# S5 stage of a two-layer trunk on one core: half of the first tokens prepared inside the last GEMM, tile 0's outputs computed with channels on the partitions, gelus of tiles 2 and 3 apart, u gathered at odd steps

## The chip, the cores and the metric

One of the eight cores of a Trainium2 chip runs the whole program. The metric is the device time of one execution in microseconds, taken as the median over runs of the same kernel; smaller is better.

## What is computed

Two layers over 256 tokens of width 2048, in float32. The change lies in the mixer of the second layer, an S5 block, and at the end of the MLP ahead of it:

```python
def rmsnorm(x, g):
    y = xf * lax.rsqrt(jnp.mean(xf * xf, axis=-1, keepdims=True) + EPS)
    return y * g

def s5_mixer(h, ...):                 # 128 groups of 16 channels, 64 complex states each
    u = h.reshape(B, S, S5_GROUPS, S5_GROUP)
    ...
    bu_re = einsum('sgc,gpc->sgp', u_s, bb_re); bu_im = ...
    x_re, x_im = associative_scan(_scan_combine, (a, bu), axis=0)
    y = einsum('sgp,gcp->sgc', x_re, cr) - einsum('sgp,gcp->sgc', x_im, ci)
    y = y + d_skip * h
    g = gelu(y)
    val, gate = split(g @ w_glu, 2, axis=-1)
    return val * sigmoid(gate)

x = x + sqrelu_mlp(rmsnorm(x, norm_mlp[0]), ...)     # layer 0 ends
x = x + s5_mixer(rmsnorm(x, norm_mix[1]), ...)       # layer 1 begins
```

The factor of the rmsnorm of a token is known only when its whole row of x is there, so nothing of S5 that needs the factor can start before the last GEMM of the MLP has given that token's last 512 channels.

## The kernel before, in words

Every large product is a GEMM on TensorE (PE) in which 128x128 blocks of weights, or of the transposed activations, stand still and 512 columns stream past them. A weight chunk is loaded by the DMA queue of SyncE (SP), and ScalarE (ACT, line 191) and VectorE (DVE, line 113) split it into a high and a low part; three products of such parts make one.

The last GEMM ahead of S5 is `gemm_skewed` (line 299): its second half goes through the tokens 0 to 127 (t = 0) first and calls `done0` (line 1276) for them, then through the tokens 128 to 255 (t = 1) and calls it again. `done0` squares and sums the row (ACT) and gets the rstd of the 128 tokens (DVE and ACT, `Norm.finish`).

`s5_phase` (line 1129) works through 16 tiles j of 128 channels (8 groups). The 256 tokens are 64 chunks k of 4 tokens each. Per tile:

- u: `s5_u` (line 1022) brings two tiles at once into the layout that the next products want. TensorE writes the tokens transposed, and scaled by rstd, into a PSUM bank (line 1031), and 16 small ScalarE copies gather it (line 1036). Tiles 0 to 3 are gathered before the rstd is known and scaled later by `s5_scale` (line 1043). Their factor is a small product (line 1141) of two selection tables with the rstd.
- e: `s5_e` (line 1049) multiplies u with the input tables on TensorE (line 1056, 16 calls, each with 64 columns of weights), and VectorE turns the result by the phase tables, scans it over k (line 1066) and turns it back into the states X[j].
- y: `s5_y` (line 1078) sums u and the states into the outputs on TensorE (line 1089, 24 calls). ScalarE takes the gelu, 16 small instructions (line 1096) for one tile or, with twice the columns each, for a group of two, then casts the result (line 1100).
- glu: `glu_tile` (line 1116) multiplies the gelu of a tile with its rows of the GLU weights (line 1122), accumulating over tiles in four banks. It runs some tiles behind: tiles 0 and 1 at steps 2 and 3, tile i at step i + 3 after that (`LAG`).

Each engine runs its queue in the order in which the program names the instructions. In the loop over j that is: e of tile j+1, glu of an earlier tile, y of tile j, a ScalarE copy for the scan's decay (line 1020), the gelus when j ends a group, then, at j = 2, 4, 6, 8, u of the tiles j+6 and j+7. `keep_warm` (line 320) adds TensorE products whose result nobody reads (`WARM` = 18, 4 and 8 of them at three kinds of places).

The banks matter. In this stage e and u (from tile 8 on) share two PSUM banks in turn:

```python
cut(4)
rings["sd"], rings["y"] = [4, 5], [6, 7]
def bank():
    return ring("sd")      # s5_e, and s5_u with kind="sd"
```

A product that takes a bank waits until its last user, two calls back, has been read: an e by VectorE (line 107), a u by the last of ScalarE's 16 copies.

Of the kernel before, what the change touches and what calls it, by code (L numbers as in the profile page):

```python
# [38 lines left out]
Q = 4  # L39

SLOTS_HOP = 3
WARM = (18, 4, 8)
LAG = 3


# [12 lines left out]
def tile_trunk(  # L58
# [69 lines left out]
    def spawn(gen, delay=0):  # L128
        side.append([clock[0] + delay, gen])
# [892 lines left out]
    def s5_u(j, diag=None, kind="sd"):  # L1022

        ps = ring(kind).rearrange("p (i s) -> p i s", s=S)
        for i in range(2):
            for t in range(NT):
                o, xs = ps[:, i, t * P:(t + 1) * P], xres[t][:, (j + i) * P:(j + i + 1) * P]
                if diag is None:
                    pe.transpose(o, xs, ident)
                else:  # L1030
                    pe.matmul(o, xs, diag[:, t], start=True, stop=True)
        u = tmp([P, 2, Q, NCH], "vsb", bufs=4)
        pv = ps.rearrange("p i (k s) -> p i s k", s=L)
        for s in range(L):
            for q in range(Q):
                act.copy(u[32 * s:32 * s + 32, :, q], pv[32 * q:32 * q + 32, :, L - 1 - s])  # L1036
            yield s
        if diag is None:
            U[j] = u
        else:  # L1040
            U[j], U[j + 1] = u[:, 0], u[:, 1]

    def s5_scale(j, factor):
        u = U[j]
        uv = u.rearrange("p i q k -> p (i q) k")
        mult(uv, uv, factor[:, None, :].broadcast_to([P, 2 * Q, NCH]))
        U[j], U[j + 1] = u[:, 0], u[:, 1]

    def s5_e(j):
        te, to, tt, ct = tab[j]  # L1050
        u, dk, xp = U[j], dks[j % 4], xps[j % 4]
        pe_ = bank().rearrange("p (i q k) -> p i q k", i=2, q=Q)
        for i in range(2):
            for q in range(Q):
                for h in (slice(0, GP), slice(GP, P)):
                    pe.matmul(pe_[h, i, q], te[:, i, q, h], u[:, q], start=True, stop=True)
        sh = [P, 2, Q, NCH]
        tw = tmp([P, 2] + sh[1:], "c5")
        t1, t2 = tw[:, 0], tw[:, 1]
        mult(t1, pe_, ct[:, 0:1].broadcast_to(sh))  # L1060
        mult(t2, pe_, ct[:, 1:2].broadcast_to(sh))
        add(t1[:, 0], t1[:, 0], t2[:, 1])
        sub(t1[:, 1], t1[:, 1], t2[:, 0])
# [12 lines left out]
        X[j] = xp

    def s5_y(grp):

        n = len(grp)  # L1080
        py = ring("y").rearrange("p (j q k) -> p j q k", j=2, q=Q)
        for jj, j in enumerate(grp):
            te, to, tt, ct = tab[j]
            u, xp = U[j], X[j]
            for q in range(Q):
                terms = ((tt[:, q], u[:, q]), (to[:, 0, q], xp[:, 0, q]), (to[:, 1, q], xp[:, 1, q]))
                for m, (w_, d) in enumerate(terms):
# [28 lines left out]
    def glu_tile(j):  # L1116
# [3 lines left out]
        for i, accs in ((c, A["v"]), (c + 1, A["g"])):  # L1120
# [4 lines left out]
            if kk == WK - 1:  # L1125
                load_next()
                pos[0] += 1

    def s5_phase(norm):
# [3 lines left out]
        sel = wp.tile([P, 2, NT, P], F32, tag="wl", name="sel", bufs=LIVE)  # L1133
        ar, diag = sel[:, 0], sel[:, 1]
        for t in reversed(range(NT)):
            tsc(ar[:, t], sela.rearrange("p s r -> p (s r)"), norm.rstd[:, t:t + 1], ALU.mult)
        for t in range(NT):
            act.activation(diag[:, t], ident, AF.Copy, scale=norm.rstd[:, t:t + 1])
        prs = bank()[:, 0:NCH]
        for t in range(NT):  # L1140
            pe.matmul(prs, ar[:, t], selb[:, t], start=(t == 0), stop=(t == NT - 1))
        keep_warm(WARM[1])
        s5_scale(0, prs)
        s5_scale(2, prs)
        s5_e(0)
        for j in (4, 6):
            for _ in s5_u(j, diag, "acc"):
                pass
        groups = [(0,), (1,), (2, 3), (4, 5), (6, 7), (8, 9), (10, 11), (12, 13), (14,), (15,)]
        ys = {}  # L1150
        for grp in groups:
            gen = s5_y(grp)
            for j in grp:
                ys[j] = (gen, j == grp[-1])
        glu = 0
        for j in range(NJ):
            if j + 1 < NJ:
# [12 lines left out]
            if end:  # L1170
                for _ in gen:
                    pass
            if j in (2, 4, 6, 8):
                for _ in s5_u(j + 6, diag):
                    pass
            s5_fetch(j + 4)
            pump()
        while glu < NJ:
            prep(GLU0 + 16 + glu - NJ + LAG)
            glu_tile(glu)  # L1180
            glu += 1
        s5_rest(NJ)
# [212 lines left out]
```

## Time and profile before

| | |
|---|---|
| median of 3 runs | 2104.44 us (2101.5, 2104.44, 2106.57) |
| profiled execution, its own time | 2101.04 us |
| its span, first to last instruction | 2099.3 us |
| TensorE busy | 2076.1 us, 99% of the span |
| VectorE, ScalarE, GpSimd busy | 1369.1, 1061.4, 122.9 us |
| granted TensorE clock, mean | 0.999 |

The profile is one execution on the chip. A timeline row gives the start in us from the span's first instruction, the us from the first start to the last end of the merged instructions, the engine, the line of the kernel, the operation, the tiles (out<-in), shapes, the count, and in brackets how long the engine sat idle before and what ended it. Ends of matmuls are modelled, so the time that a product takes from the queue is read as the distance between two starts. An fp32 product shows as two matmul rows.

### The profile page before, as it was taken

How to read it: one execution, taken by the hardware profiler on the slowest of the kernel's cores; microseconds unless marked ns; L12 is line 12 of the kernel's file. 1: busy time of each engine (PE TensorE's matmuls, PEld its weight loads, DVE VectorE, ACT ScalarE, POOL GpSimd, SP SyncE). 2: the span in 40 equal slices, each digit the busy share in tenths (PEclk: the TensorE clock that was granted, in tenths of full speed). 3: DMA queues.
4: the chain of work that ended last, by engine and by line, in shares of the span. 5: the costliest groups of instructions: out<-in, count | busy, mean ns of one | idle time of the engine just before them, and what ended most of it. 6: DMA issues, size and time to landing. Idle time of an engine off the chain costs nothing.

```text
span 2099.3 us, 31788 instructions
## 1 busy us (share of the span) xinstructions
PE 2076.1 (99%) x12126; PEld 1763.8 (84%) x12126; DVE 1369.1 (65%) x2292; ACT 1061.4 (51%) x1640; POOL 122.9 (6%) x210
## 2 busy tenths in 40 slices
PE   8999999999999999999999999999999999999998
PEld 8899998888888888888887668888888888888886
DVE  5785656688678767767866865565556645645655
ACT  5545545555445444454566875444434434434443
POOL 2000200021021002100110000000000000000000
PEclk9999999999999999999999999999999999999999
DMA  7457765677776777687678765665565556555653
GB/s 244 157 193 241 248 178 184 214 229 267 237 240 233 273 238 222 225 276 235 208 266 310 274 215 187 200 201 199 189 195 189 189 193 191 178 204 181 200 192 131
DMA packets 230813, 452.57 MB, mean 216 GB/s; under 512 B 20818, under 2 KB 29348, under 8 KB 230660
## 3 DMA queue, kind: packets, MB, share of 16 engines
q1 hardware_dynamic: 217824, 415.29, 59.8%
q0 software_dynamic: 11440, 32.86, 4.9%
q10 hardware_dynamic: 1396, 2.39, 0.3%
q8 instruction: 95, 1.56, 0.3%
q14 instruction: 58, 0.48, 0.1%
HBM read 420.85 MB, written 41.68 MB: 220 GB/s over the span
## 4 chain that ended last, share of the span: by engine, by line
PE 91%; ACT 3%; DVE 3%; DMA 1%; issue 1%; SPq 0%; DVEq 0%; ACTq 0%
PE acc L265 21%; PE acc L201 15%; PE acc L202 15%; PE acc L203 15%; PE acc L269 11%; PE acc L1122 3%; PE acc L248 2%; PE acc L250 2%; PE acc L249 2%; DVE wl L113 1%; ACT wh L191 1%; PE y L1089 1%; ACT s2k L1096 1%; DMA raw<-in_a_w_in_dram 1%; ACT vsb L1036 1%
## 5 line engine op out<-in xcount | busy, mean ns | idle before, releaser
L113 DVE TENSOR_TENSOR wl<-raw,wh 128x1024 fp32r<-128x1024 f32 (+1 forms) x690 | 833.2, 1217 | 574.4 <-ACT wh L191 570.0
L191 ACT CAST wh<-raw 128x1024 fp32r<-128x1024 f32 (+1 forms) x690 | 712.9, 1047 | 631.0 <-PE acc L203 341.4
L201 PE MATMUL acc<-wh,x 128*128 128x512 f32 x832 | 326.8, 393 | 0.0
L203 PE MATMUL acc<-wh,x 128*128 128x512 f32 x832 | 324.0, 389 | 0.0
L202 PE MATMUL acc<-wl,x 128*128 128x512 f32 x832 | 324.0, 389 | 0.0
L265 PE MATMUL acc<-x,wh 128*128 128x512 f32 x1024 | 273.9, 394 | 2.8 <-DVE s2k L110 2.8
L265 PE MATMUL acc<-a,wh 128*128 128x512 f32 x1024 | 272.8, 393 | 0.0
L201 PE MATMUL acc<-wh,a 128*128 128x512 f32 x640 | 251.5, 393 | 0.0
L202 PE MATMUL acc<-wl,a 128*128 128x512 f32 x640 | 249.4, 390 | 0.1
L203 PE MATMUL acc<-wh,a 128*128 128x512 f32 x640 | 249.3, 390 | 0.0
L265 PEld LDWEIGHTS acc<-x,wh 128*128 128x128 f32 x1024 | 177.3, 189 | 28.9 <-DVE s2k L110 3.2
L265 PEld LDWEIGHTS acc<-a,wh 128*128 128x128 f32 x1024 | 177.3, 189 | 25.3 <-ACT s2k L1324 0.4
L203 PEld LDWEIGHTS acc<-wh,x 128*128 128x128 f32 x832 | 156.2, 188 | 32.9
L201 PEld LDWEIGHTS acc<-wh,x 128*128 128x128 f32 x832 | 156.3, 188 | 32.0 <-ACT vsb L1317 0.3
L202 PEld LDWEIGHTS acc<-wl,x 128*128 128x128 f32 x832 | 156.3, 188 | 31.8 <-issue 0.2
L269 PEld LDWEIGHTS acc<-a,wl 128*128 128x128 f32 x1024 | 152.8, 190 | 18.7
L269 PEld LDWEIGHTS acc<-x,wl 128*128 128x128 f32 x1024 | 152.4, 190 | 18.8
L269 PE MATMUL acc<-x,wl 128*128 128x256 f32 x1024 | 158.0, 282 | 0.0
L269 PE MATMUL acc<-a,wl 128*128 128x256 f32 x1024 | 157.5, 281 | 0.0
L248 PE MATMUL acc<-x,wh 128*128 128x256 f32 x512 | 148.4, 290 | 1.2 <-ACT wh L191 1.2
L249 PE MATMUL acc<-x,wh 128*128 128x256 f32 x512 | 145.4, 284 | 0.1
L250 PE MATMUL acc<-x,wl 128*128 128x256 f32 x512 | 145.5, 284 | 0.0
(246 smaller groups left out, 2105.8 us busy)
## 6 DMA issues: line engine op xcount, KB each, us to landing
raw<-in_mlp_w_dram SPq DMA_DIRECT2D x512, 512.0 KB
raw<-in_a_w_in_dram SPq DMA_DIRECT2D x94, 512.0 KB
raw<-in_b_w_glu_dram SPq DMA_DIRECT2D x64, 512.0 KB
raw<-in_a_w_out_dram SPq DMA_DIRECT2D x32, 512.0 KB
scr<-t POOLq DMA_DIRECT2D x32, 512.0 KB, 5.6
teo<-scr SPq DMA_DIRECT2D x32, 512.0 KB
t<-scr SPq DMA_DIRECT2D x16, 512.0 KB
pwr<-pwn SPq DMA_DIRECT2D x16, 256.0 KB
```

The lines of the kernel that those rows point to most:

```text
L113: v.tensor_tensor(out=o, in0=a, in1=b, op=ALU.subtract)
L191: act.copy(h[:, sl], r[:, sl])
L201: pe.matmul(accs[t], lhs.h[:, k, ts], wh, start=first, stop=False)
L202: pe.matmul(accs[t], lhs.h[:, k, ts], wl, start=False, stop=False)
L203: pe.matmul(accs[t], lhs.l[:, k, ts], wh, start=False, stop=last)
L248: pe.matmul(o, wh[:, kk, cs], lhs.h[:, k], start=f and c % 2 == 0, stop=False)
L249: pe.matmul(o, wh[:, kk, cs], lhs.l[:, k], start=False, stop=False)
L250: pe.matmul(o, wl[:, kk, cs], lhs.h[:, k], start=False, stop=e and c % 2 == 1)
L265: pe.matmul(a[c], wh, lhs.hl[:, k].rearrange("p i s -> p (i s)"), start=first, stop=False)
L269: pe.matmul(a[c][:, S:], wl, lhs.h[:, k], start=False, stop=last)
L1036: act.copy(u[32 * s:32 * s + 32, :, q], pv[32 * q:32 * q + 32, :, L - 1 - s])
L1122: pe.matmul(accs[t], g[:, t * P:(t + 1) * P], raws[i][:, kk], start=j == 0, stop=j == NJ - 1)
```

## The change

`s5_e` is cut into `s5_in` (TensorE), `s5_turn` and `s5_sums` (VectorE) and `s5_states` (VectorE), the first three of which can do half of the chunks k, that is the tokens of t = 0 or of t = 1. `s5_scale` can do halves too.

- The factor for t = 0 and the scaling of tiles 0 to 3 for it move into the last GEMM (`s5_ahead`, started when `done0` has the rstd of t = 0). After that GEMM's last product, ahead of the rstd of t = 1, come e's products of tiles 0 and 1 for t = 0, and tile 0's turn.
- `s5_phase` then does the other halves, for tile 0 ahead of the loop, for tile 1 at j = 0. `WARM` becomes (11, 2, 8).
- Tile 0's outputs come from `s5_y_direct`: the weights have 32 columns, each product writes 32 partitions, so that channels lie on the partitions and one ScalarE gelu takes the tile.
- Tiles 2 and 3 are groups of their own: 32 gelus on 64 columns instead of 16 on 128.
- u of the tiles 8 to 15 is gathered at the end of the steps j = 1, 3, 5, 7 instead of 2, 4, 6, 8.

```diff
-WARM = (18, 4, 8)
+WARM = (11, 2, 8)
...
+    def s5_in(j, ks=ALL):
+        te, u = tab[j][0], U[j]
+        pe_ = banks[j] = bank().rearrange("p (i q k) -> p i q k", i=2, q=Q)
         for i in range(2):
             for q in range(Q):
                 for h in (slice(0, GP), slice(GP, P)):
-                    pe.matmul(pe_[h, i, q], te[:, i, q, h], u[:, q], start=True, stop=True)
+                    pe.matmul(pe_[h, i, q, ks], te[:, i, q, h], u[:, q, ks], start=True, stop=True)
...
+    def s5_y_direct(j):
+        te, to, tt, ct = tab[j]
+        u, xp = U[j], X[j]
+        py = ring("y")[:, 0:S].rearrange("p (s k) -> p s k", s=L)
+        for s in range(L):
+            cs = slice(32 * s, 32 * s + 32)
+            for q in range(Q):
+                terms = ((tt[:, q], u[:, q]), (to[:, 0, q], xp[:, 0, q]), (to[:, 1, q], xp[:, 1, q]))
+                for m, (w_, d) in enumerate(terms):
+                    pe.matmul(py[32 * q:32 * q + 32, s], w_[:, cs], d, start=m == 0, stop=m == 2,
+                              tile_position=(0, 32 * q))
...
+        act.activation(g[:, 0].rearrange("p (k s) -> p s k", s=L), py, AF.Gelu_apprx_tanh)
...
+    def s5_ahead(norm):
+        yield from s5_factor(norm, 0)
+        s5_scale(0, prs[0], HALF[0])
+        s5_scale(2, prs[0], HALF[0])
...
+        for _ in s5_factor(norm, 1):
+            pass
+        s5_sums(0, HALF[0])
         keep_warm(WARM[1])
-        s5_scale(0, prs)
-        s5_scale(2, prs)
-        s5_e(0)
+        s5_scale(0, prs[0], HALF[1])
+        s5_in(0, HALF[1])
+        s5_turn(1, HALF[0])
+        s5_sums(1, HALF[0])
+        s5_scale(2, prs[0], HALF[1])
+        s5_turn(0, HALF[1])
+        s5_sums(0, HALF[1])
+        s5_states(0)
...
-        groups = [(0,), (1,), (2, 3), (4, 5), (6, 7), (8, 9), (10, 11), (12, 13), (14,), (15,)]
+        groups = [(0,), (1,), (2,), (3,), (4, 5), (6, 7), (8, 9), (10, 11), (12, 13), (14,), (15,)]
...
-            if j in (2, 4, 6, 8):
-                for _ in s5_u(j + 6, diag):
+            if j in (1, 3, 5, 7):
+                for _ in s5_u(j + 7, diag):
...
     def done0(u, ts):
         norm2.block(u, ts)
+        if u == NB - 1 and ts[0] == 1:
+            for j in range(2):
+                s5_in(j, HALF[0])
+            s5_turn(0, HALF[0])
```

The order of DMA issues on SP's queue stays the same, and so does GpSimd's.

First place, TensorE around u of the tiles 8 and 9 (the two L1031 rows on xres_76 and xres_77 are repeated once just ahead), before. `sd` is a bank of the pair, `teo_11850` holds the tables of tile 4, and `[waits ...]` names the engines and DMA queues that an instruction waits for.

```order
L1031 MATMUL sd_12014<-sel,xres_77 128x128
L1056 MATMUL sd_12041<-vsb_11726,teo_11850 64x64 [waits DMAHW5_49,DVE_49,PE_49]
L1056 MATMUL sd_12041<-vsb_11726,teo_11850 64x64 x15
L1122 MATMUL acc_11980<-raw_11498,s2k_11926 128x512 [waits Activation_49]
L1122 MATMUL acc_11981<-raw_11498,s2k_11926 128x512
L1122 MATMUL acc_11982<-raw_11516,s2k_11926 128x512
L1122 MATMUL acc_11983<-raw_11516,s2k_11926 128x512
```

The same place with the change; `teo_11899` holds the tables of tile 3.

```order
L1031 MATMUL sd_11988<-sel,xres_77 128x128
L1063 MATMUL sd_12015<-vsb_11233,teo_11899 64x64 [waits DMAHW0_49,DVE_49,PE_49]
L1063 MATMUL sd_12015<-vsb_11233,teo_11899 64x64 x15
L1170 MATMUL acc_12046<-raw_11498,s2k_11890 128x512 [waits DMAHW5_49,Activation_49]
L1170 MATMUL acc_12047<-raw_11498,s2k_11890 128x512
L1170 MATMUL acc_12048<-raw_11516,s2k_11890 128x512 [waits DMAHW6_49]
L1170 MATMUL acc_12049<-raw_11516,s2k_11890 128x512 [waits PE_49]
```

The u is followed by e of tile 3 now and by e of tile 4 before, so the next e, of tile 4, is the one that takes the bank of that u.

Second place, TensorE at e of tile 4 with the change: the last rows of y of tile 2 ahead, glu of tile 1 and the first row of y of tile 3 behind.

```order
L1114 MATMUL y_12054<-bc_11353,teo_11566 64x64 x4
L1063 MATMUL sd_12103<-vsb_11762,teo_11894 64x64 [waits DMAHW5_49,PE_49,Activation_49]
L1063 MATMUL sd_12103<-vsb_11762,teo_11894 64x64 x15
L1170 MATMUL acc_12046<-raw_11498,s2k_11970 128x512
L1170 MATMUL acc_12047<-raw_11498,s2k_11970 128x512
L1170 MATMUL acc_12048<-raw_11516,s2k_11970 128x512
L1170 MATMUL acc_12049<-raw_11516,s2k_11970 128x512
L1114 MATMUL y_12143<-vsb_11233,t_2137_11900 64x64 [waits DMAHW2_49]
```

Its wait for ScalarE ("Activation") is for the last copy of u of the tiles 8 and 9. The e of tiles 6, 8 and 10 have the same wait, for u of the tiles 10, 12 and 14; before, it stood at the e of tiles 5, 7, 9 and 11.

Third place, ScalarE from the gelus of tile 1 on, before (`s2k` is the gelu, `x` its cast, `s1k` the decay copy, `vsb` the gathered u):

```order
L1096 ACTIVATE s2k_11926<-y_11900 32x64 x16
L1100 CAST x_11848<-s2k_11926 128x256
L1020 COPY s1k_11352<-rr 128x4x63
L1036 COPY vsb_12019<-sd_12014 32x2x64 x16
L1020 COPY s1k_11356<-rr 128x4x63
L1096 ACTIVATE s2k_12106<-y_11988 32x128 x16
L1100 CAST x_11848<-s2k_12106 128x2x256
L1020 COPY s1k_11344<-rr 128x4x63
L1036 COPY vsb_12192<-sd_12187 32x2x64 x16
L1020 COPY s1k_11348<-rr 128x4x63
L1096 ACTIVATE s2k_12274<-y_12161 32x128 x16
L1100 CAST x_12291<-s2k_12274 128x2x256
```

With the change, from the gelus of tile 1 on:

```order
L1121 ACTIVATE s2k_11970<-y_11944 32x64 x16
L1125 CAST x_11892<-s2k_11970 128x256
L1036 COPY vsb_11993<-sd_11988 32x2x64 x16
L1020 COPY s1k_11352<-rr 128x4x63
L1121 ACTIVATE s2k_12080<-y_12054 32x64 x16
L1125 CAST x_11892<-s2k_12080 128x256
L1020 COPY s1k_11356<-rr 128x4x63
L1121 ACTIVATE s2k_12169<-y_12143 32x64 x16
L1125 CAST x_11892<-s2k_12169 128x256
L1036 COPY vsb_12192<-sd_12187 32x2x64 x16
L1020 COPY s1k_11344<-rr 128x4x63
L1020 COPY s1k_11348<-rr 128x4x63
```

The 16 copies of a u stood behind a decay copy, one step away from the gelus of a group; they now stand directly behind the gelus and the cast of the tile or group that ends at that step.

## Rows read from the trace of the kernel before

**Rows 1.** Timeline, TensorE, lead-in of S5 and its first steps.
```profile
1129.73 4.24 PE L326 MATMUL acc<-x 128*128 128x512 f32 x18
1133.81 0.55 PE L1141 MATMUL sd<-selb,sel 128*128 128x64 f32 x4
...
1136.36 2.05 PE L1031 MATMUL acc<-sel,xres 128*128 128x128 f32 x16
...
1151.27 3.70 PE L1122 MATMUL acc<-raw,s2k 128*128 128x512 f32 x8 [1.78 <-ACT s2k L1096]
...
1157.54 1.15 PE L1056 MATMUL sd<-vsb,teo 128*64 128x64 f32 x32
...
1170.52 3.70 PE L1122 MATMUL acc<-raw,s2k 128*128 128x512 f32 x8 [2.15 <-ACT s2k L1096]
```

**Rows 2.** Timeline, ScalarE, from the copies of tiles 4 to 7 on.
```profile
1137.56 8.57 ACT L1036 COPY vsb<-acc 32x128 f32<-32x128 f32 x32 [3.15 <-PE acc L1031]
...
1146.57 4.64 ACT L1096 ACTIVATE s2k<-y 32x64 f32<-32x64 f32 x16
1151.25 0.40 ACT L1100 CAST x<-s2k 128x256 fp32r<-128x256 f32 x1
...
1189.50 6.56 ACT L1096 ACTIVATE s2k<-y 32x128 f32<-32x128 f32 x16 [1.11 <-PE y L1089]
...
1196.61 0.40 ACT L1020 COPY s1k<-rr 128x252 f32<-128x252 f32 x1
```

**Rows 3.** Timeline, TensorE, steps 6 to 9 of the loop.
```profile
1182.03 1.16 PE L1031 MATMUL sd<-sel,xres 128*128 128x128 f32 x8
1183.12 1.15 PE L1056 MATMUL sd<-vsb,teo 128*64 128x64 f32 x32
1184.20 3.70 PE L1122 MATMUL acc<-raw,s2k 128*128 128x512 f32 x8
1187.83 0.34 PE L1089 MATMUL y<-vsb,t 128*64 128x64 f32 x4
...
1189.28 1.10 PE L1056 MATMUL sd<-vsb,teo 128*64 128x64 f32 x32
1190.31 3.70 PE L1122 MATMUL acc<-raw,s2k 128*128 128x512 f32 x8
...
1196.58 1.15 PE L1056 MATMUL sd<-vsb,teo 128*64 128x64 f32 x32
```

**Rows 4.** Timeline, VectorE, lead-in of S5.
```profile
1134.40 1.28 DVE L107 TENSOR_TENSOR vsb<-vsb,sd 128x512 f32<-128x512 f32 x2 [1.13 <-PE sd L1141]
...
1137.80 0.42 DVE L110 TENSOR_TENSOR c<-c 128x256 f32<-128x256 f32 x1
1138.14 0.42 DVE L113 TENSOR_TENSOR c<-c 128x256 f32<-128x256 f32 x1
```

**Rows 5.** Line 927 (32 columns of weights): ns min/median/max of one; then its timeline.
```profile
L927 PE MATMUL sd<-c,t x256: 218/219/244, 402.6 to 1043.7; 128*32 128x64 f32 x128
...
402.62 0.43 PE L927 MATMUL sd<-c,t 128*32 128x64 f32 x16
```

**Rows 6.** Timeline, TensorE, the last product of the program.
```profile
2089.48 0.39 PE L203 MATMUL acc<-wh,x 128*128 128x512 f32 x1
```

**Rows 7.** Busy time by stretch: each engine, then granted clock, DMA share, GB/s.
```profile
2090.00:2095.00 5.00, 0.00 (x0) 0.00 (x0) 3.14 (x10) 1.65 (x4) 1.25 (x1) 0.90 0.49 181
```

**Rows 8.** Timeline, TensorE, the start of the program.
```profile
7.85 0.58 PE L248 MATMUL acc<-x,wh 128*128 128x256 f32 x1 [1.24 <-ACT wh L191]
...
9.81 0.41 PE L249 MATMUL acc<-x,wh 128*128 128x256 f32 x1
10.02 0.41 PE L250 MATMUL acc<-x,wl 128*128 128x256 f32 x1
...
11.93 0.28 PE L249 MATMUL acc<-x,wh 128*128 128x256 f32 x1
12.05 0.28 PE L250 MATMUL acc<-x,wl 128*128 128x256 f32 x1
```

More of the change, by code (lines that the diff above doesn't have):

```diff
@@ L1041, in s5_u, with s5_scale @@
             U[j], U[j + 1] = u[:, 0], u[:, 1]
[L1043 to L1052, printed above, removed]
+    ALL = slice(0, NCH)
+    HALF = (slice(0, NCH // 2), slice(NCH // 2, NCH))
+    def s5_scale(j, factor, ks=ALL):
+        u, first = (U[j], True) if (j, 0) not in U else (U[j, 0], False)
+        uv = u.rearrange("p i q k -> p (i q) k")[:, :, ks]
+        mult(uv, uv, factor[:, None, ks].broadcast_to([P, 2 * Q, ks.stop - ks.start]))
+        if first:
+            U[j, 0] = u
+            U[j], U[j + 1] = u[:, 0], u[:, 1]
+    banks, turns = {}, {}
+    def s5_in(j, ks=ALL):
+        te, u = tab[j][0], U[j]
+        pe_ = banks[j] = bank().rearrange("p (i q k) -> p i q k", i=2, q=Q)
         for i in range(2):
@@ L1055, in s5_e, with s5_turn, s5_sums, s5_states @@
                 for h in (slice(0, GP), slice(GP, P)):
-                    pe.matmul(pe_[h, i, q], te[:, i, q, h], u[:, q], start=True, stop=True)
-        sh = [P, 2, Q, NCH]
[L1058 to L1063, printed above, removed]
+                    pe.matmul(pe_[h, i, q, ks], te[:, i, q, h], u[:, q, ks], start=True, stop=True)
+    def s5_turn(j, ks=ALL):
+        ct, pe_ = tab[j][3], banks.pop(j)
+        if j not in turns:
+            turns[j] = tmp([P, 2, 2, Q, NCH], "c5")
+        sh = [P, 2, Q, ks.stop - ks.start]
+        for m in range(2):
+            mult(turns[j][:, m, :, :, ks], pe_[:, :, :, ks], ct[:, m:m + 1, :, ks].broadcast_to(sh))
+    def s5_sums(j, ks=ALL):
+        t1, t2 = turns[j][:, 0], turns[j][:, 1]
+        add(t1[:, 0, :, ks], t1[:, 0, :, ks], t2[:, 1, :, ks])
+        sub(t1[:, 1, :, ks], t1[:, 1, :, ks], t2[:, 0, :, ks])
+    def s5_e(j):
+        s5_in(j)
+        s5_turn(j)
+        s5_sums(j)
+        s5_states(j)
+    def s5_states(j):
+        ct, dk, xp = tab[j][3], dks[j % 4], xps[j % 4]
+        t1 = turns.pop(j)[:, 0]
+        sh = [P, 2, Q, NCH]
         zz = tmp(sh, "s2k", bufs=7)
@@ L1103, in s5_y @@
         rest.append((grp[-1], blk, kk, n, g))
+    def s5_y_direct(j):
[9 more added lines that the diff above has]
+                              tile_position=(0, 32 * q))
+        yield j
+        del U[j], X[j], tab[j]
+        g = tmp([P, 2, S], "s2k", bufs=7)
+        act.activation(g[:, 0].rearrange("p (k s) -> p s k", s=L), py, AF.Gelu_apprx_tanh)
+        blk, kk = glu_lhs[j // KB], j % KB
+        if blk.h is None:
+            new_lhs(blk, "x")
+        act.copy(blk.h[:, kk:kk + 1], g[:, 0:1])
+        G[j] = g[:, 0]
+        rest.append((j, blk, kk, 1, g))
     rest = []
@@ L1127, in glu_tile, with s5_factor @@
                 pos[0] += 1
+    sels, prs = [], []
+    def s5_factor(norm, t):
+        if t == 0:
+            sels.append(wp.tile([P, 2, NT, P], F32, tag="wl", name="sel", bufs=LIVE))
+            prs.append(ring("acc")[:, 0:NCH])
+        ar, diag = sels[0][:, 0], sels[0][:, 1]
+        tsc(ar[:, t], sela.rearrange("p s r -> p (s r)"), norm.rstd[:, t:t + 1], ALU.mult)
+        act.activation(diag[:, t], ident, AF.Copy, scale=norm.rstd[:, t:t + 1])
+        if t == 0:
+            yield 2
+        pe.matmul(prs[0][:, HALF[t]], ar[:, t], selb[:, t, HALF[t]], start=True, stop=True)
+    def s5_ahead(norm):
+        yield from s5_factor(norm, 0)
+        s5_scale(0, prs[0], HALF[0])
+        s5_scale(2, prs[0], HALF[0])
     def s5_phase(norm):
@@ L1132, in s5_phase @@
         keep_warm(WARM[0])
[L1133 to L1141, printed above, removed]
-        keep_warm(WARM[1])
-        s5_scale(0, prs)
-        s5_scale(2, prs)
-        s5_e(0)
+        for _ in s5_factor(norm, 1):
+            pass
+        s5_sums(0, HALF[0])
+        keep_warm(WARM[1])
+        s5_scale(0, prs[0], HALF[1])
[6 more added lines that the diff above has]
+        s5_states(0)
+        diag = sels[0][:, 1]
         for j in (4, 6):
@@ L1148, in s5_phase @@
                 pass
-        groups = [(0,), (1,), (2, 3), (4, 5), (6, 7), (8, 9), (10, 11), (12, 13), (14,), (15,)]
+        groups = [(0,), (1,), (2,), (3,), (4, 5), (6, 7), (8, 9), (10, 11), (12, 13), (14,), (15,)]
         ys = {}
         for grp in groups:
-            gen = s5_y(grp)
+            gen = s5_y(grp) if grp[0] else s5_y_direct(0)
             for j in grp:
@@ L1156, in s5_phase @@
         for j in range(NJ):
-            if j + 1 < NJ:
+            if j == 0:
+                s5_in(1, HALF[1])
+                s5_turn(1, HALF[1])
+                s5_sums(1, HALF[1])
+                s5_states(1)
+            elif j + 1 < NJ:
                 s5_e(j + 1)
@@ L1282, in done0 @@
             norm2.finish(slice(ts[0], ts[0] + 1))
+            if ts[0] == 0:
+                spawn(s5_ahead(norm2))
     def early_u():
```

## The prediction, made before the changed kernel ran

> **What bounds the kernel now.** I read the page first: TensorE is busy for 99% of the span, so a change outside S5's stage would have to shorten TensorE's queue. Then the timelines of the S5 stage, engine by engine, to see where TensorE sits idle there and who ends it. The reader is to see three things.
>
> First, the lead-in. The first warm product stands at 1129.73, right behind the last GEMM, and the first glu product starts at 1151.27, released by ScalarE's gelus of tile 0 after 1.78 us idle [rows 1]. ScalarE is what is late: from 1137.56 its queue is a string without gaps, 32 copies of u (8.57), a decay copy, 16 gelus of tile 0 (4.68 to the cast behind them) [rows 2].
>
> Second, the steps. Once the loop runs, TensorE has no gaps: u takes 1.09 us (start to start), e 1.03 behind a y and 1.08 behind a u, glu 3.63, y 1.45 [rows 3]. A pair of steps with one u is 1.09 + 1.08 + 1.03 + 2 x 3.63 + 2 x 1.45 = 13.36 us.
>
> Third, ScalarE's pair of steps: the gelus and the cast of a group 7.11 (1189.50 to 1196.61), 16 copies of u 4.28 (half of the 32), decay copies 0.40 each [rows 2], 12.2 us in all. That is only 1.2 us under TensorE's 13.36, so the order of this queue decides whether TensorE waits.
>
> **The change part by part.** I carry each part to one common state. When the old kernel starts e of tile 4 (1157.54 [rows 1]), u of tiles 8 and 9, glu of tile 0 and y of tile 2 have been issued; the changed kernel has the same behind it when it starts its e of tile 4. The same holds at e of tile 10 (1196.58 [rows 3]): four u, glu up to tile 5, y up to tile 8. Behind that the two kernels have the same work in the same order. So the change is worth the shift of the first point plus the change of the stretch between the two, 39.04 us before.
>
> *Warm products.* Nine fewer (7 of 18, 2 of 4) at 0.227 each (4.08 us for 18 [rows 1]) are 2.0 us of TensorE. They lay where TensorE waits for VectorE or ScalarE, so by themselves they buy nothing.
>
> *Half of the tokens early.* The factor for t = 0 costs the GEMM two more rows, about 0.2 us (half of the four rows of 1133.81 [rows 1], less a tail); its VectorE part falls into the wait for t = 1. After the GEMM come two half e, bounded by half and all of a full e (0.5 to 1.08 each); then 11 warm products, the factor, and 0.6 us to VectorE (1133.81 to 1134.40 [rows 1, 4]). That puts the first scaling of t = 1 at 1134.2 to 1135.3. VectorE then does half-size operations, 0.34 us for 256 elements from start to start [rows 4], about 0.2 for 128: scaling, turn and sums of tile 1, and the second scaling, 1.8 us in all. The second scaling is what u of tiles 4 to 7 now waits for, because the factor lies in the accumulator bank which that u takes. So that u starts at 1136.0 to 1137.1 on TensorE against 1136.36, and ScalarE's copies 1.2 us later (1136.36 to 1137.56 [rows 1, 2]): 1137.2 to 1138.3. I take 1137.7. The early halves make the states of tiles 0 and 1 ready 1 to 2 us sooner, but ScalarE's string starts no sooner.
>
> *Tile 0 with one gelu.* 16 gelus, 4.68 us, become one on 256 elements. No row shows that form. Four times the gelu on 64 elements (4 x 0.28) is the upper bound, the cast on 256 elements (0.40) the lower [rows 2]; I take 0.62, the rise per element from 64 to 128 elements drawn on. TensorE's part doubles its rows to 96, each with 32 columns of weights. Nearest are 16 rows of that form in 0.43 us, 0.22 of it the last row itself [rows 5]: 14 ns each, 1.4 us for 96. But there the calls go round the four groups of 32 columns, here three calls to one group follow each other. If nothing overlapped, a row would hold its group for some 57 ns (four times that), 5.5 us. I take 1.4, the same form of instruction, and keep 5.5 for a rival.
>
> *e of tile 4.* ScalarE's string is now: 32 copies 8.6, decay 0.4, gelu 0.6, cast 0.4, decay 0.4, gelus of tile 1 4.7, cast 0.4, copies of u of tiles 8 and 9 4.3, in all 19.8 from 1137.7, so 1157.5. With the u one step earlier, it is e of tile 4 that takes the bank of that u. TensorE's own queue from its u at 1136.5 is 2.05 for it, half an e, 8 warm 1.8, y of tile 0 1.4, e 1.03, 8 warm 1.8, y of tile 1 1.45 and a tail of 0.2, to 1147.0 or so; then u, e of tile 3, glu of tile 0 and y of tile 2 (7.25). It waits from 1154.3 to 1157.5. **The shift of the first point is 0.0**, though glu of tile 0 starts 2 us earlier, at about 1149.2: the lead-in's gain is given back as a wait of 3.2 us. The old wait of 2.15 at 1170.52 goes, too; it lies inside the stretch.
>
> *e of tiles 6, 8 and 10.* These wait for the copies of u of tiles 10, 12 and 14, and those copies now stand behind the gelus of the very y that ended the step. Each is a closed loop: e 1.03, glu 3.63, y 1.45, 0.22 until the gelus start (1189.28 to 1189.50 [rows 2, 3]), together 6.33, then gelus, cast, copies and the next such e. From tile 4 to 6 (single gelus): 6.33 + 4.68 + 0.40 + 4.28 = 15.7. From 6 to 8 and from 8 to 10 (groups): 6.33 + 7.11 + 4.28 = 17.7 each. TensorE has 9.7, 13.4 and 13.4 us of work in these (no glu at step 4), so it idles 6.0, 4.3 and 4.3 us. **The stretch becomes 51.1 us, 12.1 more.**
>
> *VectorE and DMA.* VectorE ends none of TensorE's waits in the stage now [rows 1], and the steps get longer. SP's issues keep their order; a slower stage gives transfers more time. Both at 0.
>
> *The clock.* The longest idle of TensorE inside the old program is 2.15 us, at granted clock 1.0. How it stands after 4 to 6 us the end shows: the last product ends at 2089.87 [rows 6], and the stretch from 2090 to 2095 has a mean of 0.90, one fifth of it at 0.5 [rows 7], so the clock fell to its lower level (1.2 GHz) near 2094.0, 4.2 us after TensorE stopped. The way back: from 7.85 to 11.93 products of 256 columns came every 0.213 us, then every 0.120 [rows 8]. Of 4.1 us at the lower level 1.8 are lost. The idle of 6.0 us is clearly longer than 4.2 and I count one fall, +1.8; the two of 4.3 are a coin's toss. Bounds 0 and 5.4 (three falls).
>
> The Trainium skill ("TensorE: Matmul & The Clock Gate", section on HAM oscillation) says that idle gaps between bursts of products can send the array back to the low clock each time. By that, three falls.
>
> **Sum.** 0.0 + 12.1 + 1.8 = +13.9 us. On the profiled execution's 2101.04 that is 2114.9. That execution is 3.4 us under the median of the runs shown, 2104.44; on the median the forecast is **2118.3 us**. The runs shown spread over 5 us, and about 0.2%, 4 us, is what a measurement of this kernel can tell from no change.
>
> **The rivals.**
>
> *The clock falls after every wait.* Same waits, 12.1 + 5.4 = +17.5: 2121.9. For it: 4.3 is over 4.2. Against: that is one observation, and the third wait lies on the edge. Chance 0.20.
>
> *The clock never falls.* +12.1: 2116.5. For it: TensorE works densely on either side of each wait, while at the end of the program nothing followed. Chance 0.20.
>
> *Tile 0's y is slow.* At 5.5 instead of 1.4 us, y of tile 1 ends 4.1 later; 1.1 of it is slack, since ScalarE gets to that gelu at 1148.1 only. The first point moves by 3.0, with one fall 13.9 + 3.0 = +16.9: 2121.3. It decides from 2.5 us on. For it: three calls in a row to the same columns. Against: the rows of 32-column products overlap four deep. Chance 0.15.
> The Trainium skill (same page, section on packing small matmuls) says that matmuls start and end strictly in program order, which would make this the case; rows 5 show four groups at work at once although each call makes two rows, which speaks for overtaking, at 14 ns a row.
>
> *Faster.* The copies of a u do not hold up the next e. Then only the lead-in counts: glu of tile 0 2.1 earlier with u (1.09) already done, and the wait of 2.15 gone, -5.3: 2099.1. It decides at the point where gelus, cast and copies fit into the 7.3 us that TensorE has between a y and the e that takes the bank; the rows give 9.4 for a tile and 11.4 for a group [rows 2]. They would have to be a third faster. Chance 0.03.
>
> *It does nothing.* What the waits cost, the lead-in pays: within 4 us of 2104.4. It needs two of the three loops not to close. Chance 0.02.
>
> **How the numbers follow.** The forecast as it stands has 0.40. The range starts 3 us below the case without a fall (half the spread of the runs and 0.5 for the start of the copies), 2113.5, and ends at 2122.5, just above three falls and the slow y alone; a slow y with more falls, and the two cases that are not slower, are left out. Faster by over 0.2%: 0.03. Within 0.2%: 0.03. Slower: 0.94.
>
> **What would show it.** Right: in TensorE's timeline e of tiles 4, 6, 8 and 10 (line 1063) each stands behind an idle of about 3, 6, 4.3 and 4.3 us, ended by ScalarE's copies (line 1036); from e of tile 4 to e of tile 10 51 us, more with a fall; glu of tile 0 starts near 1149.2; ScalarE's copies of tiles 4 to 7 begin near 1137.7; the granted clock is below 1.00 in a stretch behind the 6 us wait. Wrong: if these idles are missing or under 2 us, if the 32-column rows of tile 0 take over 2.5 us, or if glu of tile 0 starts later than before.

## The result, and the profile after

The changed kernel takes **2123.61 us** (median of 4 runs, 2122.69 to 2124.44), the old one 2103.68 (4 runs, 2101.5 to 2106.57): ratio 1.0099, 95% interval [1.0086, 1.0111], or 19.9 us slower. The forecast was 13.9 slower, 2118.3, and its range ended at 2122.5. The direction, the places and the cause of the waits came out as written; the size did not.

The profiled execution after has a time of 2123.44 us, a span of 2121.7 and a mean granted clock of 0.993 (before: 2101.04, 2099.3, 0.999). TensorE is busy for 2085.5 us, 98% of the span. I cut both traces at three marks on TensorE: the last row of the GEMM ahead of S5, the last glu row, and the end.

| | before | after | difference |
|---|---|---|---|
| start to the last GEMM row ahead of S5 | 1129.51 | 1131.64 | +2.13 |
| from there to e of tile 4 | 28.03 | 29.28 | +1.25 |
| e of tile 4 to e of tile 10 | 39.04 | 55.72 | +16.68 |
| e of tile 10 to the last glu row | 52.58 | 54.96 | +2.38 |
| last glu row to the end | 850.11 | 850.07 | -0.04 |

The first line is not the change's: up to there the programs differ on TensorE by two small rows, and in the twelve traces of this study the mark lies anywhere from 1128.65 to 1132.40, whatever the kernel. In this execution 1.7 of the 2.13 us is time lost to a fall of the clock in the MLP (granted clock 0.66 from 818 to 823, TensorE busy throughout; before, it is 1.00 there). The traces of experiments 7 and 10 below have the same fall, and these three have the three latest marks. The three lines of the stage make +20.3, close to the 19.9 of the medians. The GLU stage and all behind it take the same time.

The timeline of TensorE after, from the half e's of tiles 0 and 1 to e of tile 11:

```profile
1131.97 2.06 PE L1063 MATMUL sd<-vsb,teo 128*64 128x32 f32 x64
1133.96 2.80 PE L326 MATMUL acc<-x 128*128 128x512 f32 x11
...
1139.03 2.02 PE L1031 MATMUL acc<-sel,xres 128*128 128x128 f32 x16 [0.49 <-DVE vsb L107]
1140.98 1.12 PE L1063 MATMUL sd<-vsb,teo 128*64 128x32 f32 x32
1142.04 2.11 PE L326 MATMUL acc<-x 128*128 128x512 f32 x8
1144.07 0.30 PE L1140 MATMUL y<-vsb,t 128*32 128x64 f32 x2
...
1146.65 1.15 PE L1063 MATMUL sd<-vsb,teo 128*64 128x64 f32 x32
...
1153.49 3.70 PE L1170 MATMUL acc<-raw,s2k 128*128 128x512 f32 x8
...
1160.92 1.15 PE L1063 MATMUL sd<-vsb,teo 128*64 128x64 f32 x32 [2.18 <-ACT vsb L1036]
1162.00 3.70 PE L1170 MATMUL acc<-raw,s2k 128*128 128x512 f32 x8
...
1176.75 1.97 PE L1063 MATMUL sd<-vsb,teo 128*64 128x64 f32 x32 [5.93 <-ACT vsb L1036]
1178.66 4.72 PE L1170 MATMUL acc<-raw,s2k 128*128 128x512 f32 x8
...
1196.52 1.98 PE L1063 MATMUL sd<-vsb,teo 128*64 128x64 f32 x32 [4.24 <-ACT vsb L1036]
1198.42 5.08 PE L1170 MATMUL acc<-raw,s2k 128*128 128x512 f32 x8
...
1216.64 1.98 PE L1063 MATMUL sd<-vsb,teo 128*64 128x64 f32 x32 [4.25 <-ACT vsb L1036]
1218.55 5.25 PE L1170 MATMUL acc<-raw,s2k 128*128 128x512 f32 x8
...
1225.18 1.10 PE L1063 MATMUL sd<-vsb,teo 128*64 128x64 f32 x32
```

The e of tiles 4, 6, 8 and 10 are the four rows with a bracket ended by line 1036, ScalarE's copies of u. In [rows 1, 3] no e has a bracket at all. Behind the last three of these waits e itself takes 1.97 or 1.98 us instead of 1.15, and the glu behind it 4.7 to 5.3 instead of 3.70: TensorE comes out of the wait slow. From e to e it is 15.83, 19.77 and 20.12, and from e of tile 10 to that of tile 11 8.54 (before 6.16, from 1196.58 [rows 3] to 1202.74).

What TensorE waited for between 1130 and 1275, in all, how often, and the longest:

```profile
PE sd L1063 <- ACT vsb L1036: 16.6, 4, 5.9
PE acc L1170 <- ACT s2k L1121: 0.5, 1, 0.5
PE acc L1031 <- DVE vsb L107: 0.5, 1, 0.5
```

The granted clock in six stretches in and behind these waits (stretch, length, TensorE's busy time and rows, granted clock, DMA share, GB/s):

```profile
1173.00:1174.00 1.00, 0.00 (x0) 0.96 0.88 283
1174.00:1175.00 1.00, 0.00 (x0) 0.50 1.03 348
...
1177.00:1180.00 3.00, 3.00 (x34) 0.50 0.42 167
1180.00:1182.00 2.00, 2.00 (x5) 0.81 0.00 0
...
1194.00:1195.00 1.00, 0.00 (x0) 0.70 1.08 358
...
1214.00:1215.00 1.00, 0.00 (x0) 0.94 0.96 315
```

So the clock goes to its lower level, 1.2 GHz, inside each of the three long waits, and TensorE then works at that level for some microseconds (3.00 us of 3.00 busy at 0.50).

ScalarE, whose queue sets all this, against [rows 2]:

```profile
1140.19 8.60 ACT L1036 COPY vsb<-acc 32x128 f32<-32x128 f32 x32 [3.81 <-PE acc L1031]
...
1149.24 0.63 ACT L1145 ACTIVATE s2k<-y 128x256 f32<-128x256 f32 x1
...
1151.44 4.67 ACT L1121 ACTIVATE s2k<-y 32x64 f32<-32x64 f32 x16 [0.82 <-PE y L1114]
...
1156.58 4.29 ACT L1036 COPY vsb<-sd 32x128 f32<-32x128 f32 x16
...
1167.30 4.66 ACT L1121 ACTIVATE s2k<-y 32x64 f32<-32x64 f32 x16 [0.59 <-PE y L1114]
...
1172.42 4.28 ACT L1036 COPY vsb<-sd 32x128 f32<-32x128 f32 x16
```

The copies of tiles 10 and 11 stand at 1172.42, behind the gelus of tile 3 that the y of the same step released. They end at 1176.70, and e of tile 6 starts at 1176.75. That is the closed loop of the forecast. New against the forecast is the bracket of 0.82 at the gelus of tile 1: y of tile 1 was late.

### The profile page after: what moved, and what is told of

Its sections match the earlier page's. It is cut to its first block, busy times and chain, and to the rows that moved or that the text cites. A ratio compares the mean times of both kernels' runs of the same rounds, so it can differ in the third digit from the quotient of the medians.

```text
span 2121.7 us, 32009 instructions
## 1 busy us (share of the span) xinstructions
PE 2085.5 (98%) x12229; PEld 1770.4 (83%) x12229; DVE 1370.9 (65%) x2303; ACT 1061.3 (50%) x1642; POOL 123.1 (6%) x210
## 4 chain that ended last, share of the span: by engine, by line
PE 92%; ACT 3%; DVE 2%; DMA 1%; issue 1%; SPq 0%; DVEq 0%; ACTq 0%
PE acc L265 21%; PE acc L202 15%; PE acc L201 15%; PE acc L203 15%; PE acc L269 11%; PE acc L248 3%; PE acc L250 3%; PE acc L249 3%; PE acc L1170 2%; ACT s2k L1121 1%; DVE wl L113 1%; ACT vsb L1036 1%; PE y L1114 1%; PE sd L1063 1%; ACT wh L191 1%
```

## The experiments

All ten runs beside the marks above. "Stage" is from the last GEMM row ahead of S5 to the last glu row of the profiled execution, "rest" from there to the end.

| kernel | median us | ratio to before [95%] | stage | rest |
|---|---|---|---|---|
| before | 2103.68 | | 119.65 | 850.11 |
| the change | 2123.61 | 1.0099 [1.0086, 1.0111] | 139.96 | 850.07 |
| 1 old, odd steps alone | 2131.13 | 1.0132 [1.0119, 1.0146] | 146.67 | 850.08 |
| 2 change, even steps | 2101.42 | 0.9995 [0.9986, 1.0004] | 120.01 | 850.08 |
| 3 waits filled too full | 2122.85 | 1.0096 [1.0082, 1.0110] | 140.22 | 850.10 |
| 4 change, u in its own bank | 2102.84 | 1.0001 [0.9992, 1.0010] | 117.78 | 853.13 |
| 5 waits filled | 2116.87 | 1.0068 [1.0056, 1.0080] | 133.47 | 850.09 |
| 6 row groups in turn | 2121.39 | 1.0087 [1.0074, 1.0100] | 140.95 | 850.14 |
| 7 even, own bank, leaner | 2101.59 | 0.9993 [0.9984, 1.0002] | 115.81 | 853.18 |
| 8 old, odd, own bank | 2105.49 | 1.0008 [0.9999, 1.0016] | 119.94 | 853.30 |
| 9 as 7, bank returned | 2097.53 | 0.9978 [0.9967, 0.9988] | 115.79 | 850.06 |
| 10 as 4, bank returned | 2100.10 | 0.9985 [0.9976, 0.9994] | 117.75 | 850.09 |

The kernel before ran beside each group; its median there was 2103.21 (1 to 4), 2103.00 (5 to 8) and 2103.01 (9 and 10).

**Experiment 1: the odd steps alone.** The old kernel with

```
-            if j in (2, 4, 6, 8):
-                for _ in s5_u(j + 6, diag):
+            if j in (1, 3, 5, 7):
+                for _ in s5_u(j + 7, diag):
```

> The old kernel with one edit: u of tiles 8 to 15 at the odd steps 1, 3, 5, 7; lead-in, groups and warm products as before. Theory A (the closed loops over u's PSUM bank, and the clock that falls in each long wait, make the loss): ScalarE's string puts the copies of u of tiles 8 and 9 behind gelu and cast of tile 1, so they end near 1160.6 and e of tile 4 starts at 1160.8 instead of 1157.5 (+3.3); then three loops with groups, 17.7 us each, 53.1 against 39.0 (+14.1), and at least two falls of the clock at 2.3 us: +22 to +24, about 2126 to 2128. Rival B (a good part of the measured loss of 20 comes from the lead-in: half e's, 32-column rows, the two rows in the GEMM): the odd steps alone cost clearly less than the whole change, under +15, so under 2119.

2131.13, 27.9 over before. One part of the change costs more than the whole of it, so the rest of the change (the new lead-in and the single gelus of tiles 2 and 3) gives something back and does not cost. Its timeline of TensorE, the four e behind the copies:

```profile
1162.57 1.97 PE L1056 MATMUL sd<-vsb,teo 128*64 128x64 f32 x32 [4.92 <-ACT vsb L1036]
...
1181.98 1.98 PE L1056 MATMUL sd<-vsb,teo 128*64 128x64 f32 x32 [7.99 <-ACT vsb L1036]
...
1201.99 1.98 PE L1056 MATMUL sd<-vsb,teo 128*64 128x64 f32 x32 [4.27 <-ACT vsb L1036]
...
1222.22 1.97 PE L1056 MATMUL sd<-vsb,teo 128*64 128x64 f32 x32 [4.26 <-ACT vsb L1036]
```

Here all four e come out at 1.97 or 1.98, so four falls where I had counted two or more; at 2.3 us each the two more make most of the 4 us above theory A's upper figure. Rival B falls. In the first of these waits the clock fell late: TensorE stopped at 1157.65 (1162.57 less 4.92), and the granted clock is

```profile
1158.00:1161.00 3.00, 0.00 (x0) 1.00 0.57 175
1161.00:1163.00 2.00, 0.43 (x8) 0.88 0.00 0
```

0.88 over two us is 0.5 us at 0.50, so it fell near 1162.5, 4.9 us after TensorE stopped.

**Experiment 2: the even steps again.** The changed kernel with the same two lines turned back; lead-in and single gelus stay.

> The changed kernel with one edit undone: u of tiles 8 to 15 at the even steps 2, 4, 6, 8 again; all of the new lead-in stays. Theory A: the waits of 5.9, 4.2 and 4.2 us and all falls of the clock go. What is left is the lead-in: glu of tile 0 starts a little earlier than before (-0.8, since u no longer stands ahead of it), the old wait of 2.15 for the gelus of tiles 2 and 3 goes, but with single gelus the copies of u of tiles 8 and 9 stand behind the gelus of tile 2 and e of tile 5 waits about 2.3 us for their bank. Sum -1 or so: 2101 to 2105. Rival B (the lead-in itself costs): 2108 or more.

2101.42. The loss is gone, all of it, with the new lead-in still there: rival B falls a second time. The wait that theory A put in the old one's place is there as well, at e of tile 5:

```profile
1164.59 1.15 PE L1063 MATMUL sd<-vsb,teo 128*64 128x64 f32 x32 [2.16 <-ACT vsb L1036]
...
1167.94 1.83 PE L1031 MATMUL sd<-sel,xres 128*128 128x128 f32 x8
```

**Experiments 3 and 5: the waits filled with products.** The changed kernel with products of a 128x128 tile that nobody reads, in the free bank of y, ahead of the e that waits (first try; in the second the counts are 6, 16, 14, 14):

```
+    def fill(n):
+        o = psum.tile([P, 512], F32, tag=f"bank{rings['y'][(turn['y'] + 1) % 2]}", name=nm("fill"), bufs=1)
+        for _ in range(n):
+            pe.matmul(o[:, 0:P], xres[0][:, 0:P], ident, start=True, stop=True)
...
+                if j in (3, 5, 7, 9):
+                    fill({3: 10, 5: 36}.get(j, 25))
                 s5_e(j + 1)
```

> The changed kernel with extra products whose result nobody reads: 10, 36, 25 and 25 products of 128 columns (0.136 us each, 1.4, 4.9, 3.4 and 3.4 us) ahead of e of tiles 4, 6, 8 and 10, into the free bank of y, so that they run while TensorE waits for ScalarE's copies. They leave about 0.8 us of each wait open. Theory A (the three stretches of 6.8 us at the lower clock are a cost of their own, 2.1 to 2.4 us each): the granted clock stays at 1.0 there, the loops take 15.8, 17.7 and 17.7 us, and the time falls by 6 to 7 us: 2116.5 to 2117.5. Rival C (the clock only fell while nothing was to be done, and what counts is ScalarE's string): within 2 us of 2123.6.

2122.85, as rival C had it, but the run decides nothing. I had taken 0.136 us for one product, and it makes two rows of about that:

```profile
1156.77 2.50 PE L1180 MATMUL fill<-ident,xres 128*128 128x128 f32 x20
```

So the fill was twice as long as the waits: no e waited for a copy any more, the fill itself was the wait. The second try has the lengths right.

> The filled waits again with about half as many products, since a product of 128 columns in this form makes two rows and takes 0.25 us (20 rows in 2.50 us in the run with 10): 6, 16, 14 and 14 of them, 1.5, 4.0, 3.5 and 3.5 us, ahead of e of tiles 4, 6, 8 and 10, so that they end 0.5 to 0.8 us before ScalarE's copies. Theory A (the falls of the clock are a cost of their own): granted clock 1.0 through the stage, e to e 15.8, 17.7 and 17.7 us with ScalarE's copies ending each wait, and 6 to 7 us less than the changed kernel: 2116.5 to 2117.5. Rival C (the falls cost nothing beyond the waits): e to e stays near 15.8, 19.8 and 20.1 and the time within 2 us of 2123.6.

2116.87, 6.7 under the changed kernel; the stage of the trace is 6.5 shorter. TensorE at e of tiles 6, 8 and 10, each now behind a wait for the same copies, but a short one:

```profile
1174.59 1.15 PE L1063 MATMUL sd<-vsb,teo 128*64 128x64 f32 x32 [0.90 <-ACT vsb L1036]
...
1192.51 1.15 PE L1063 MATMUL sd<-vsb,teo 128*64 128x64 f32 x32 [0.92 <-ACT vsb L1036]
...
1210.42 1.15 PE L1063 MATMUL sd<-vsb,teo 128*64 128x64 f32 x32 [0.91 <-ACT vsb L1036]
1211.50 3.70 PE L1170 MATMUL acc<-raw,s2k 128*128 128x512 f32 x8
```

and the stretch in which e of tile 8 waits, granted clock 1.00:

```profile
1188.00:1194.00 6.00, 5.08 (x71) 1.00 0.97 355
```

The copies end each wait as before, so ScalarE's string is unchanged; from e to e it is 15.81, 17.92 and 17.91 (forecast without clock: 15.7, 17.7, 17.7), then 6.16. What went is the slow e (1.97) and the slow glu (4.7 to 5.3). Theory A holds: the falls are a cost of their own, on top of the waits, 6.5 us for three.

**Experiments 4 and 8: a bank for u alone.** From step 1 on e has one of the two banks and u the other. Experiment 4 is the changed kernel, experiment 8 the old kernel with odd steps, each with

```
+            if j == 1:
+                rings["sd"], rings["u"], turn["sd"], turn["u"] = [4], [5], 0, 0
...
-                for _ in s5_u(j + 7, diag):
+                for _ in s5_u(j + 7, diag, "u"):
```

> The changed kernel, u still at odd steps, but with a PSUM bank of its own from step 1 on, and e with the other one alone. Theory A (it is the shared bank that ties e to ScalarE's copies, not that u itself comes too late): the four waits go, since ScalarE's pair of steps (12.2 us) is shorter than TensorE's (13.4); u of tiles 12 and 13 may wait 0.7 us for its bank. From glu of tile 0 to e of tile 10 some 42.8 us against 45.3 before; the time comes to 2101 to 2104. Rival D (the copies are late as such, for e of tile 8 needs u itself and the y bank is held by late gelus): waits of 3 us or more move to other lines, and the time stays over 2112.

> The old kernel with u at odd steps and a PSUM bank for it alone: old lead-in, tiles 2 and 3 as a group. Theory A: as in the changed kernel the bank is the whole tie, so the loss of 28 us that odd steps alone gave goes; what stays are waits for gelus (0.7 at glu of tile 1, some 2 at glu of tile 2): 2103 to 2107. Its distance to the changed kernel with its own bank (2102.8) is then what the new lead-in and single gelus are worth when nothing takes it back: 0 to 4 us. Rival D (with the old lead-in, 1.5 to 2 us later on ScalarE, the copies come too late for e of tile 8 itself): over 2110.

2102.84 and 2105.49, both within theory A's figures and the noise of the old kernel's time: the loss from u at odd steps is gone once e no longer takes its bank. In experiment 4 the one wait left is the one that theory A named, u of tiles 12 and 13 for its own bank, 1.36 instead of 0.7:

```profile
1173.28 1.16 PE L1031 MATMUL u<-sel,xres 128*128 128x128 f32 x8 [1.36 <-ACT vsb L1036]
```

Rival D falls in both lead-ins. The stages, 117.78 and 119.94, differ by 2.2 us, but 1.7 of that is one slow glu in experiment 8, behind a wait of 1.88 us (5.40 instead of 3.70, last section), and the intervals of the two medians overlap. What the new lead-in and the single gelus are worth with nothing to take it back is some 2 us at most by these stages, and not told from nothing here. In both, and in experiment 7, which leaves the same bank behind, the rest is 3 us longer than in the other kernels, though, and the waits of TensorE behind the stage show why:

```profile
PE sd L461 <- DVE a L122: 2.4, 3, 0.8
```

My edit left the ring of e with one bank after S5, and the transposes of the GLU stage (line 461) use that ring.

**Experiment 6: the row groups in turn.** The changed kernel with the loops of tile 0's y exchanged:

```
-            for q in range(Q):
-                ...
-                for m, (w_, d) in enumerate(terms):
+            for m, (w_, d) in enumerate(((tt, u), (to[:, 0], xp[:, 0]), (to[:, 1], xp[:, 1]))):
+                for q in range(Q):
```

> The changed kernel with the 96 rows of tile 0's y in another order: for each column group s and each of the three terms the four row groups in turn, instead of three terms in a row to one row group. If three calls in a row to the same 32 columns are what made a row take 26 ns, the 96 rows now take 1.3 to 1.5 us (14 ns each, as the rows of line 927 do) instead of 2.5; y of tile 1 ends 1.1 earlier and the gelus of tile 1 lose their wait of 0.82, and with them the first closed loop starts 0.8 earlier: 2122.8. If the form itself takes 26 ns a row, all stays as it was: 2123.6.

The rows, the first of them, and the e that follows the last:

```profile
1141.08 0.32 PE L1139 MATMUL y<-vsb,t 128*32 128x64 f32 x8
...
1142.56 1.15 PE L1063 MATMUL sd<-vsb,teo 128*64 128x64 f32 x32
```

1.48 us from the first row to the next e, against 2.58 (1144.07 to 1146.65) in the changed kernel: 15 ns a row instead of 27. So the order of the calls is the cause. In the old order three calls in a row go to one group, and they also add into the same outputs; no run here tells which of the two it is. The wait of 0.82 at the gelus of tile 1 goes, and e of tile 4 comes 28.30 us behind the last GEMM row instead of 29.28. In the profiled execution the gain does not last: TensorE stopped at 1166.85 ahead of e of tile 6 (1172.77, after 5.92 idle), the clock fell only 5.4 us later and 0.6 us ahead of that e (0.61 over the us below is 0.8 us at 0.50), and behind the falls glu takes 5.85, 5.64 and 5.55 us here; the stage is 1.0 longer than the changed kernel's.

```profile
1172.00:1173.00 1.00, 0.23 (x4) 0.61 1.01 414
```

The ratios of the medians, 2121.39 and 2123.61, to the old kernel have overlapping intervals; whether this edit alone pays is open.

**Experiments 7, 9 and 10: versions to beat both.** 7 puts together the new lead-in, u at even steps in its own bank, the row groups in turn, and 5 instead of 8 warm products at step 0. 9 and 10 are 7 and 4 with the bank returned:

```
         s5_rest(NJ)
+        rings["sd"], turn["sd"] = [4, 5], 0
```

> A version meant to beat both: the new lead-in, u at the even steps with a PSUM bank of its own from step 1, the rows of tile 0's y in turn over the row groups, and 5 instead of 8 warm products at step 0. Against the run with u at the even steps: its wait of 2.2 us for the copies of u of tiles 8 and 9 goes or becomes 0.7 at u of tiles 10 and 11, and glu of tile 0 starts 1 to 2 us earlier. 2098 to 2100; if VectorE's states (x of tile 1 ready some 4.5 us after x of tile 0) hold y of tile 1 longer than I read, 2100 to 2101.

> The version with u at even steps, its own bank and fewer warm products, with one line more: behind S5 the transposes of the GLU stage get both banks back. In the run without it the stage itself (last GEMM row to last glu row) was 115.8 us against 119.7 before, but the rest of the program took 852.8 us against 850.0, with three waits of 0.8 us at the transposes for VectorE. If the single bank left over is the cause of the 2.8 us, the rest is 849.4 to 850.0 again and the time 2098 to 2099.5, 4 to 5 us under the old kernel. If the rest is longer for another reason (a shorter S5 that meets the weights' transfers), it stays at 2101 to 2102.

> The changed kernel with u at odd steps in a bank of its own, and the same line more: both banks back for the transposes behind S5. Stage 117.8 us as in the run without the line, the rest 849.5 to 850 instead of 853.0: 2099.5 to 2101, so 2 to 3 us under the old kernel with u still at odd steps.

7 came to 2101.59, above both figures, and not by VectorE: its stage is 3.8 us shorter than before, and 3.1 of that go back at the transposes. (By the marks of the table the rest is 853.18 in 7 and 850.11 before, where the expectation of 9 has 852.8 and 850.0.) With the bank returned the rest is 850.06 and the time 2097.53, a little below the expected 2098 to 2099.5 and 5.5 us under the old kernel beside it (ratio 0.9967 to 0.9988). 10, still with u at odd steps, is at 2100.10, 2.9 under, within its figures. The largest wait of TensorE left in the stage of 9 is for the gelus of tiles 4 and 5:

```profile
1179.62 3.70 PE L1169 MATMUL acc<-raw,s2k 128*128 128x512 f32 x8 [1.42 <-ACT s2k L1121]
```

## Why the prediction was wrong in size

**Right: the mechanism.** e of tiles 4, 6, 8 and 10 wait for ScalarE's copies, with 2.18, 5.93, 4.24 and 4.25 us idle against 3, 6, 4.3 and 4.3. That the tie is the shared bank, experiments 2, 4 and 8 show: take u back to even steps, or away from e's bank, and nothing of the loss remains. Without the clock the three loops take 15.81, 17.92 and 17.91 (experiment 5), 51.64 in all; that is 12.6 more than the 39.04 of before, where 12.1 stood.

**The step that failed: the clock.** "The idle of 6.0 us is clearly longer than 4.2 and I count one fall, +1.8; the two of 4.3 are a coin's toss." All three waits brought the clock down, and each fall cost more than 1.8. From 19.77 and 20.12 against experiment 5's 17.92 and 17.91, and 8.54 against 6.16, a fall cost 1.9, 2.2 and 2.4 us, in all 6.4 where 1.8 stood (upper bound 5.4).
Both the count and the price were taken from one observation each. At the end of the program the clock fell 4.2 us after the last product [rows 6, 7]. Here it fell 3.1, 2.1 and 2.5 us after TensorE stopped (at 1173.9, 1194.4 and 1214.9; TensorE stopped at 1170.82, 1192.28 and 1212.39, the starts of e less the idle), but 4.9 us after in the first long wait of experiment 1 and 5.4 in that of experiment 6. So there is no fixed delay to compare a wait with; what the traces do show is that all ten waits of 4.2 us or more (three here, four in experiment 1, three in experiment 6) brought the clock down.
The price was taken from a stretch of 4.1 us of products at the lower level [rows 8], while the loss is half of what TensorE works at that level. In the first fall that was 4.0 us (from e at 1176.75 until about 1180.8: 0.81 from 1180 to 1182), in the other two up to 5 us. In experiment 6, whose first fall came just ahead of e, a fall cost 2.7 to 3.0 us.
The Trainium skill ("TensorE: Matmul & The Clock Gate", section on HAM oscillation) says that gaps between bursts can send the array back to the low clock each time; by that there were to be three falls. The trace agrees: the three waits here, from 4.24 us, and the four of experiment 1, from 4.26 us, all brought it down.

**Also missed: the first point.** Forecast 0.0, measured +1.25. ScalarE's copies begin 8.55 us behind the last GEMM row, against 8.05 before and a forecast of 8.2 (inside the bounds, but late: each half e took 0.99 us, near the upper end of "0.5 to 1.08"). Then the gelus of tile 1 waited 0.82 for y of tile 1, since the 96 rows of tile 0 took 2.58 us, not 1.4. That is the rival "tile 0's y is slow", just past the point from which I had said that it decides. With fast rows (experiment 6) the wait of 0.82 is gone. By the forecast's slack of 1.1 these rows should have cost only 0.1; the slack had been used up by the rows of TensorE ahead of them, which were late too. The Trainium skill ("TensorEngine Tiling (Array Packing)", Key Properties) says that different tiles of the array can work in parallel. The 15 ns a row of calls that go round the groups, against 27 ns with three calls in a row to one group, agree with that. That rows 5 "speak for overtaking" was read into them: they show rows that overlap, not one that passes another. Glu of tile 0 came 21.85 us behind the last GEMM row (1153.49), no earlier than before (21.76), where I had 2 us earlier. So two of the prediction's own signs of being wrong came, this one by 0.09 us and the rows of tile 0 by 0.08. With fast rows it is 20.75 (1149.40 in experiment 6), so half of that error is the slow y. The rest lies in TensorE's other rows: the half e behind u took 1.06 (1140.98 to 1142.04) where 0.5 stood, the eight warm products 2.03 (1142.04 to 1144.07) where 1.8 stood, and u itself began 0.4 late. None of these was tried by itself.

**The sum again:** 1.25 + 12.6 + 6.4 = 20.3, as the stage has it. The nearest rival was the one in which the clock falls after every wait, 2121.9. With the first point it comes to 2123.2, within 0.5 of the measured time, but part of that is luck: it adds 18.8 us where the stage shows 20.3, and the median of 2104.44 that it starts from is 0.8 above the 2103.68 beside the result. The range failed because its upper end took three falls without a late first point, and at my own price of 1.8.

## What to carry to other kernels

- When a producer is moved a step earlier, look at which queue it then stands in and which ring of buffers it takes: here u went behind gelus in ScalarE's queue while its bank was the next but one for e, and TensorE had to wait for a queue that was not short of time. A buffer of its own for the producer cured it without moving anything back; give the buffer back to the ring behind the loop.
- A wait of TensorE of 4.2 us or more inside dense work cost itself and, in all ten cases here, 1.5 to 3.0 us of slow products behind it (from e to e, against experiment 5). Price both, for every wait, and do not read the second price from one place.
- Small column-group products want neighbouring calls to go to different groups, which here also meant different outputs: 15 ns a row against 27.

## What the runs showed of the hardware that was not expected

Waits of 2 us can bring the clock down too, and behind them, not inside. In the MLP of the profiled execution after, outside the change, TensorE waited 2.19 us and the clock fell 1.5 us after it had resumed (TensorE's row, then two of the stretches):

```profile
817.45 0.73 PE L265 MATMUL acc<-x,wh 128*128 128x512 f32 x2 [2.19 <-DVE s2k L110]
```

```profile
818.00:819.00 1.00, 1.00 (x8) 0.97 1.06 410
819.00:820.00 1.00, 1.00 (x5) 0.50 1.05 389
```

The same happened behind the 1.88 us of experiment 8, where the glu takes 5.40 instead of 3.70 us,

```profile
1170.85 5.40 PE L1122 MATMUL acc<-raw,s2k 128*128 128x512 f32 x8 [1.88 <-ACT s2k L1096]
```

```profile
1171.00:1172.00 1.00, 1.00 (x2) 0.78 1.03 410
1172.00:1175.00 3.00, 3.00 (x5) 0.50 0.99 391
```

and behind the 2.16 us of experiment 2 (the u that took 1.83). It did not happen behind the 2.15 us of the old kernel [rows 1], whose glu takes 3.70, nor behind the 2.18 us at 1160.92 above. Counted over all twelve traces, behind the first 15 us of each, TensorE waits 17 times for 1.5 to 2.3 us. Behind five of these waits the clock fell (1.79, 1.88, 2.08, 2.16 and 2.19 us, the fall 0.5 to 1.5 us after TensorE had resumed), behind twelve it did not, the longest of them 2.30 us in experiment 6. What tells these apart no run here settles; it may be part of the 5 us by which executions of one kernel differ, which was not tried.

Halving the moving columns saved TensorE next to nothing: 64 rows of 32 columns took 1.99 us (1131.97 to 1133.96), 31 ns each, and rows of 64 columns take 32 to 34 ns (32 rows in 1.03 to 1.08 us [rows 3]). So preparing half of the tokens ahead nearly doubles TensorE's time for e of those tiles.
